# Layer 1 projections: the last key chunk's stores queued behind the last norm powers, and the eighth weight block's splits queued behind evictions

## The chip, the cores and the metric

The kernel runs as one launch on one core of a Trainium2 chip. The metric is the device time of one execution in microseconds (us), the median of several runs. The engines named here are TensorE (PE, matmuls; PEld its weight loads), VectorE (DVE), ScalarE (ACT), GpSimd (POOL) and SyncE (SP, which here only issues DMAs). Each engine runs its own list of instructions in order, and waits at an instruction until the semaphores that it names have been raised by other engines or by DMAs that have landed.

## The reference

A two-layer backbone works on T = 2304 tokens, 256 of context and 2048 latent ones on a grid of 32 rows and 64 columns, with D = 1024 channels. Layer 0 has two groups of heads, latent attention and bidirectional gated linear attention. Layer 1, in which the change lies, is a two-dimensional neighbourhood attention over 16 heads of 64. Cut to what matters:

```python
def odd_mixer(h, hc, w_in, q_gain, k_gain, rpb, w_out, update_ctx):   # layer 1; h: latent, hc: context tokens
    def heads(u):
        q, k, v, z = jnp.split(u, 4, axis=-1)
        return rms_norm(sh(q), q_gain), rms_norm(sh(k), k_gain), sh(v), z   # sh: 16 heads of 64
    q_x, k_x, v_x, z_x = heads(jnp.dot(h, w_in))
    q_c, k_c, v_c, z_c = heads(jnp.dot(hc, w_in))
    o = neighborhood_attention(q_x, k_x, v_x, k_c, v_c, rpb)   # windows of 8 rows x 16 columns, and the context
    y = jnp.dot(o.reshape(h.shape[0], h.shape[1], C_WIDTH) * jax.nn.silu(z_x), w_out)
    ...
```

So layer 1 needs the product of all token tiles with a 1024 x 4096 weight, and an RMS norm of every head of q and k. The kernel keeps k in two layouts: `K1`, from which it finds the maxima of the score rows, and `K1t`, which the attention itself reads later.

## The kernel before, in words

**Tiles and blocks.** Tokens are 18 tiles of 128 (tiles 0 and 1 are the context). The weight `w_od` is eight blocks of 512 columns: 0 and 1 are q, 2 and 3 are k, 4 and 5 are v, 6 and 7 are the gate z. One *cell* (t, j) multiplies tile t by block j: `mm3_steps` (L124) splits each fp32 factor into a high and a low part and makes three products (L129, L130, L131) for each of eight slices of D, 24 matmuls of 128 x 512, into a PSUM tile `gm`.

**Weights.** Four places w0 to w3 in SBUF hold the blocks: 2 and 4 share w0, 3 and 5 w1, 0 and 6 w2, 1 and 7 w3. A block is brought by `od_steps` (L1115) with `split_steps` (loop at L383): eight loads `wraw` of 256 KB by SP (L388) through a few staging buffers, each split into a high part by ACT (`w0h` to `w3h`, the activation of L106) and a low part by DVE (`w0l` to `w3l`, L391). When the last cell of blocks 2, 3, 0, 1 is through, `done(j)` appends block 4, 5, 6, 7 to the list `self.ahead`, from which `pump` takes a step at every fourth matmul step.

**Stage odd_qk (L1122)** runs q and k: cells in the order j = 2, 3, 0, 1 for each tile, the last two tiles (16 and 17) together, so that it ends (16,2), (17,2), (16,3), (17,3), (16,0), (17,0), (16,1), (17,1), and then (16,4), (17,4), the first two cells of v. Behind each q or k cell stands the norm: squares on ACT (`osq`), sums on DVE (`oss`, L1156), scale and power -1/2 on POOL (`rpow`, L208 and L210), the product on DVE (`onat`, L1159). A later cell's sixth step then calls `fin` (L1163): four PE transposes into `tp` (L1167), `oqh` and `oql` from them, stores to K (`K1`) or Q by SP. For k, `fin` also fills `okt`, the second layout in high and low parts, a chunk of 512 tokens (four tiles) at a time; when a chunk's last tile is in, `store_k` (L1196) issues four stores of 512 KB from POOL to `K1t` (L1200), for j = 2 and for j = 3. The last chunk's eight stores so stand on POOL among the powers of tiles 16 and 17. The two v cells evict to `onat` by ACT (L1150) and store to V1 from POOL (`store_v`, L1215, DMA at L1222).

**Stage odd_vz (L1224)** runs the rest of v and z with the tiles reversed: (17,5), (16,5), (17,6), (16,6), (17,7), (16,7), (15,4) and so on. Its pools take over memory that odd_qk's pools gave back. Block 5's cells evict to `ovz` by ACT and store to V1; z's are a tanh on ACT, a product on DVE (`ovz`, L1248) and PE transposes (L1251). Woven into them is `maxes`, row maxima of the scores per head: a key tile `mk` (1152 KB, from K), a table `mtab` (899 KB) to which POOL adds two masks (L1279, L1280), a query piece `mq`, spread by ACT into `mz` (zeroed by DVE, L1260), matmuls into `mx`, and reductions on DVE into `mm` (set by L1282).

**Order.** A framework orders each engine's instructions by its own forecast of a timeline. `issue_after(ins)` adds to that: what is issued inside it, on the same engine as `ins`, comes behind `ins`. `held(steps)` (L158) runs steps inside `issue_after(self.evicted.ins)`, so that ACT splits come behind the eviction kept in `self.evicted`. DMAs issued from POOL share one queue, and the compiled program takes eight completion counters in turn for them: a DMA waits for the one that used its counter before, eight DMAs earlier.

Of the kernel before, what the change touches and what calls it, by code (L numbers as in the profile page):

```python
# [13 lines left out]
ALU = mybir.AluOpType  # L14
# [7 lines left out]
CTX = 256  # L22
T = SEQ + CTX
NT = T // P
NCT = CTX // P
EPS = 1e-6
# [62 lines left out]
class Kern:  # L89
# [115 lines left out]
    def rpow(self, out, in_, mul, add):  # L205

        g = self.nc.gpsimd
        g.tensor_scalar(out=out, in0=in_, scalar1=mul, scalar2=add, op0=ALU.mult, op1=ALU.add)  # L208
        shp = list(out.shape)
        g.tensor_tensor(out=out, in0=out, in1=self.mhalf[:, : shp[1]], op=ALU.pow)  # L210


    def consts(self, es):
# [908 lines left out]
    def odd_qk(self, ws, win, hT):  # L1122
        nc = self.nc
        self.V1c = self.scr("V1c", (2, P, NCT, 512), F32)
        self.V1 = self.scr("V1", (2, SEQ, 512), F32)
        self.Q1 = self.scr("Q1", (2, 8, P, SEQ), F32)
        self.K1 = self.scr("K1", (8, P, T), F32)
        self.K1t = self.scr("K1t", (8, 2, P, T), F32)
        with ExitStack() as es:
            sp = self.pool(es, "osA", bufs=2, side="left", reuse_waits="tile")  # L1130
            pp = self.pool(es, "opA", bufs=2, space=PSUM, reuse_waits="tile")
            qkg = self.tl(sp, [P, 2], "oqkg", bufs=1)
            nc.sync.dma_start(qkg[:], self.i["od_gain"])
            nc.vector.tensor_scalar(out=qkg[:, 0:1], in0=qkg[:, 0:1], scalar1=0.125, scalar2=None, op0=ALU.mult)
            self.ahead += [self.od_steps(win, 0, ws), self.od_steps(win, 1, ws)]
            pend, kt = [], {}

            def cell(t, j):
                hi, lo = hT[t]
                wh, wl = win[j]  # L1140
                ps = self.tl(pp, [P, 8, 64], "gm", bufs=3)
                steps = self.mm3_steps(ps[:], (lambda k: hi[:, k, :], lambda k: lo[:, k, :]),
                                       (lambda k: wh[:, k, :], lambda k: wl[:, k, :]), range(KD))
                for n, _ in enumerate(steps):
                    if n == 5 and pend and (len(pend) > 1 or j == 4):
                        fin(*pend.pop(0))
                    yield
                if j == 4:
                    n = self.tl(sp, [P, 512], "onat", bufs=4)
                    self.act(n[:], ps[:].rearrange("p h d -> p (h d)"))  # L1150
                    self.store_v(t, 0, n)
                    return
                sq = self.tl(sp, [P, 512], "osq")
                self.act(sq[:], ps[:].rearrange("p h d -> p (h d)"), AF.Square)
                ss = self.tl(sp, [P, 8], "oss", bufs=4)
                nc.vector.tensor_reduce(out=ss[:], in_=sq[:].rearrange("p (h d) -> p h d", h=8), axis=AX.X, op=ALU.add)  # L1156
                self.rpow(ss[:], ss[:], 1.0 / 64, EPS)
                n = self.tl(sp, [P, 512], "onat", bufs=4)
                nc.vector.tensor_tensor(out=n[:].rearrange("p (h d) -> p h d", h=8), in0=ps[:],  # L1159
                                        in1=ss[:].unsqueeze(2).to_broadcast([P, 8, 64]), op=ALU.mult)  # L1160
                pend.append((t, j, n))

            def fin(t, j, n):  # L1163
                z = j // 2
                ps = self.tl(pp, [P, 4, P], "tp")
                for i in range(4):
                    nc.tensor.transpose(ps[:, i, :], n[:, i * P : i * P + P], self.ident[:])  # L1167
                hi = self.tl(sp, [P, 4, P], "oqh", F32R)
                self.act(hi[:], ps[:], AF.Copy, scale=qkg[:, z : z + 1])
                j0 = (j % 2) * 4  # L1170
                if z == 1:
                    nc.sync.dma_start(self.K1[j0 : j0 + 4, :, t * P : t * P + P].rearrange("j p t -> p j t"), hi[:].bitcast(F32))
                if z == 0 or t < NCT:
                    lo = self.tl(sp, [P, 4, P], "oql", F32R)
                    nc.vector.scalar_tensor_tensor(out=lo[:], in0=ps[:], scalar=qkg[:, z : z + 1], in1=hi[:],
                                                   op0=ALU.mult, op1=ALU.subtract)
                    if z == 0:
                        for part, tt in enumerate((hi, lo)):
                            nc.sync.dma_start(self.Q1[part][j0 : j0 + 4, :, (t - NCT) * P : (t - NCT) * P + P].rearrange("j p t -> p j t"),
                                              tt[:].bitcast(F32))  # L1180
                    else:
                        store_k((hi, lo), j0, t * P, P)
                    return
                g, r0 = divmod(2 * (t - NCT), 8)
                if r0 == 0:
                    kt[j] = [self.tl(sp, [P, 4, 512], f"okt{j}{part}", F32R, bufs=1) for part in range(2)]
                view = lambda x, n: x[:].rearrange("p i (r c b) -> p i r c b", r=n, c=4)
                for r in range(2):
                    oh, ol = (x[:].rearrange("p i (c b r) -> p i r c b", c=4, r=8)[:, :, r0 + r] for x in kt[j])
                    self.act(oh, view(ps, 2)[:, :, r], AF.Copy, scale=qkg[:, z : z + 1])  # L1190
                    nc.vector.scalar_tensor_tensor(out=ol, in0=view(ps, 2)[:, :, r], scalar=qkg[:, z : z + 1],
                                                   in1=view(hi, 2)[:, :, r], op0=ALU.mult, op1=ALU.subtract)
                if r0 == 6:
                    store_k(kt.pop(j), j0, CTX + g * 512, 512)

            def store_k(parts, j0, o, w):  # L1196

                for u, x in enumerate(parts):
                    for i in range(2):
                        nc.gpsimd.dma_start(self.K1t[j0 : j0 + 4, i, u * 64 : u * 64 + 64, o : o + w].rearrange("j d t -> d j t"),  # L1200
                                            x[i * 64 : i * 64 + 64].bitcast(F32))

            nxt = {2: 4, 3: 5, 0: 6, 1: 7}
            done = lambda j: j in nxt and self.ahead.append(self.od_steps(win, nxt[j], ws))
            cells = self.cells(list(range(NT)), (2, 3, 0, 1), lambda t, j: j > 1 or t >= NCT) + [(NT - 2, 4), (NT - 1, 4)]
            for _ in self.stream(cells, hT, cell, lambda t: self.prep(1, t, self.x1, pp, ("px", 2)), done):
                self.pump()
            while pend:
                fin(*pend.pop(0))
# [14 lines left out]
    def odd_vz(self, ws, win, hT):  # L1224
# [4 lines left out]
        with ExitStack() as es:  # L1229
# [6 lines left out]
            def cell(t, j):  # L1236
                hi, lo = hT[t]
                wh, wl = win[j]
                ps = self.tl(pp, [P, 512], "gm")
                yield from self.mm3_steps(ps[:], (lambda k: hi[:, k, :], lambda k: lo[:, k, :]),  # L1240
                                          (lambda k: wh[:, k, :], lambda k: wl[:, k, :]), range(KD))
                n = self.tl(sp, [P, 512], "ovz", bufs=3)
                if j < 6:
                    self.act(n[:], ps[:])
                    self.store_v(t, j - 4, n)
                    return
                self.last_tanh = self.act(n[:], ps[:], AF.Tanh, scale=0.5)
                nc.vector.scalar_tensor_tensor(out=n[:], in0=n[:], scalar=1.0, in1=ps[:], op0=ALU.add, op1=ALU.mult)  # L1248
                pt = self.tl(pp, [P, 4, P], "tp", bufs=1)
                for i in range(4):  # L1250
                    nc.tensor.transpose(pt[:, i, :], n[:, i * P : i * P + P], self.ident[:])  # L1251
                z = self.tl(sp, [P, 4, P], "ozt", bufs=1)
                self.act(z[:], pt[:])
                o = (t - NCT) * P
                nc.scalar.dma_start(self.z1[(j - 6) * 4 : (j - 6) * 4 + 4, :, o : o + P].rearrange("j p t -> p j t"), z[:])
# [61 lines left out]

            cells = self.cells(list(range(NT))[::-1], (4, 5, 6, 7), lambda t, j: (j > 4 or t < NT - 2) and (j < 6 or t >= NCT))
            gemms = self.stream(cells, hT, cell, lambda t: self.reload(1, t))
            self.weave(gemms, maxes(), 0.57, 15)  # L1320

# [415 lines left out]
```

## Time and profile before

| what | us |
|---|---|
| median of 3 runs | 3652.93 |
| lowest, highest | 3652.69, 3655.3 |
| the profiled execution | 3652.31 |
| its span, first to last instruction | 3650.5 |
| mean granted TensorE clock, share of full | 0.988 |

The profiled execution is 1.8 us longer than its span, and 0.6 us shorter than the median. In the rows of the profile a line number is that of the kernel; a time at the start of a row is counted from the start of the span; a bracket at the end, such as [1.94 <-DVE onat L1159], tells how long the engine had been idle before and what released it. A row of the waits reads: engine and operation that waited, what it waited for, us in total, times, longest. The stages of the change lie at about 2560 to 2850 us.

### The profile page before, as it was taken

What the parts mean: (1) busy time and instruction counts of PE and PEld (TensorE: products, weight loads), DVE (VectorE), ACT (ScalarE), POOL (GpSimd) and SP (SyncE); (2) the same over time, 40 slices, a digit from 0 to 9 for tenths busy, and PEclk for the clock granted to TensorE, in tenths of its full rate; (3) what the DMA queues carried; (4) which work ended last, traced back from release to release, by engine and by line L of the source; (5) the groups of instructions that cost most, each with busy time, mean ns of one, the idle gap of its engine ahead of it and who ended that gap; (6) DMA issues with size and microseconds to landing.
All of it is one profiled execution on the core that took longest, in us unless ns stands there. A gap on an engine that the chain in (4) does not pass through costs nothing. (4 is left out here: it accounts for less than half of the span.)

```text
span 3650.5 us, 51811 instructions
## 1 busy us (share of the span) xinstructions
PE 3552.0 (97%) x18404; PEld 2747.6 (75%) x18404; DVE 2355.2 (65%) x4846; ACT 1433.2 (39%) x2740; POOL 1234.9 (34%) x1376
## 2 busy tenths in 40 slices
PE   8999999999999999999999999999899999999899
PEld 6988987888886666665656887888788887555577
DVE  4677666888876766678765435455488784666732
ACT  5445551111115555555654214444422222555510
POOL 1433330101011211221311224333344442888763
PEclk9999999999999999999999999999999999999999
DMA  7455463222243232342632544545734446898672
GB/s 259 142 156 155 135 177 110 87 75 84 69 116 86 66 107 66 89 125 66 179 110 93 184 139 141 159 146 155 245 126 144 131 133 181 212 223 220 190 235 97
DMA packets 365780, 512.25 MB, mean 140 GB/s; under 512 B 26081, under 2 KB 245297, under 8 KB 359618
## 3 DMA queue, kind: packets, MB, share of 16 engines
q1 hardware_dynamic: 320754, 417.69, 39.3%
q0 software_dynamic: 22112, 63.26, 5.7%
q10 hardware_dynamic: 22656, 27.99, 2.2%
q8 instruction: 146, 2.39, 0.3%
q14 instruction: 112, 0.92, 0.1%
HBM read 329.45 MB, written 179.37 MB: 139 GB/s over the span
## 5 line engine op out<-in xcount | busy, mean ns | idle before, releaser
L963 DVE TENSOR_TENSOR acc<-acc,apt 128x512 f32<-128x512 f32 x512 | 375.6, 756 | 168.5 <-ACT apt L106 165.6
L106 ACT ACTIVATE apt<-st 128x512 f32<-128x512 f32 (+1 forms) x592 | 343.6, 594 | 290.7 <-PE st L974 262.0
L660 DVE TENSOR_REDUCE mm<-mx 128x1 f32<-128x512 f32 (+1 forms) x656 | 388.7, 629 | 87.3 <-PE mx L659 80.0
L914 PE MATMUL av<-apt,av 128*64 128x512 f32 (+1 forms) x1184 | 280.6, 594 | 0.0
L972 PE MATMUL st<-aq,akh 97*128 97x512 f32 (+1 forms) x592 | 256.6, 434 | 8.8 <-DMA aq<-QT 4.4
L659 PE MATMUL mx<-mk,mq 96*128 96x512 f32 (+1 forms) x656 | 235.8, 373 | 5.0 <-DMA mq<-QT 3.4
L1430 POOL TENSOR_TENSOR oacc<-oacc,opt 128x576 f32<-128x576 f32 (+5 forms) x192 | 223.0, 1184 | 39.7 <-ACT rl L106 19.3
L973 PE MATMUL st<-aq,akh 96*128 96x512 f32 (+1 forms) x592 | 235.5, 398 | 0.0
L1548 DVE TENSOR_TENSOR opt<-st,tab 128x64 f32<-128x64 f32 (+10 forms) x576 | 144.6, 317 | 140.3 <-PE st L1391 63.8
L974 PE MATMUL st<-aq,akl 96*128 96x512 f32 (+1 forms) x592 | 234.4, 396 | 0.0
L106 ACT ACTIVATE u<-gm 128x352 f32<-128x352 f32 (+1 forms) x140 | 68.6, 498 | 373.2 <-PE gm L131 210.6
L1307 DVE CUSTOM_DVE_ANT_1 mx<-mx,mtab 128x217 f32<-128x217 f32 (+12 forms) x576 | 184.2, 338 | 40.1 <-PE mx L1301 30.9
L914 PEld LDWEIGHTS av<-apt,av 128*64 128x64 f32 x1184 | 80.5, 137 | 153.6 <-issue 152.3
L972 PEld LDWEIGHTS st<-aq,akh 97*128 97x128 f32 x592 | 113.0, 191 | 99.1 <-issue 50.5
L106 ACT ACTIVATE opt<-opt 128x930 f32<-128x930 f32 (+7 forms) x129 | 104.2, 810 | 110.7 <-DVE opt L1548 102.6
L659 PEld LDWEIGHTS mx<-mk,mq 96*128 96x128 f32 x656 | 121.2, 188 | 16.8 <-DMA mk<-KT 3.8
L974 PEld LDWEIGHTS st<-aq,akl 96*128 96x128 f32 x592 | 113.9, 193 | 25.6
L973 PEld LDWEIGHTS st<-aq,akh 96*128 96x128 f32 x592 | 114.4, 193 | 17.1
L129 PE MATMUL gm<-w1h,hhi 128*128 128x512 f32 x288 | 116.3, 404 | 6.8 <-ACT onat L106 6.8
L106 ACT ACTIVATE x<-px,modB,modA 128x128 f32<-128x128 f32 x272 | 99.3, 468 | 56.9 <-PE px L339 54.4
L129 PE MATMUL gm<-w0h,hhi 128*128 128x512 f32 x288 | 116.3, 404 | 2.0 <-DVE hhi L351 1.9
L807 POOL TENSOR_TENSOR gsf<-gsf,D 64x512 f32<-64x512 f32 x17 | 25.1, 1477 | 271.4 <-DVE D L784 271.4
(492 smaller groups left out, 9962.1 us busy)
## 6 DMA issues: line engine op xcount, KB each, us to landing
q<-Q SPq DMA_DIRECT2D x48, 512.0 KB
H<-x ACTq DMA_DIRECT2D x36, 512.0 KB
adaw<-ada_w SPq DMA_DIRECT2D x64, 256.0 KB
x<-H SPq DMA_DIRECT2D x32, 512.0 KB
wraw<-w_od SPq DMA_DIRECT2D x64, 256.0 KB
K1t<-okt POOLq DMA_DIRECT2D x32, 512.0 KB, 7.6
kt<-K1t SPq DMA_DIRECT2D x32, 512.0 KB
mtab<-rpb_q SPq DMA_DIRECT2D x16, 899.0 KB
```

Source lines behind the costliest of these rows:

```text
L106: return self.nc.scalar.activation(out, in_, func, **kw)
L129: self.nc.tensor.matmul(out, lh(k), rh(k), start=j == 0, stop=False)
L659: mm = nc.tensor.matmul(ps[:, :w], q[:A_QK, (t % 6) * P : (t % 6) * P + P], k[:A_QK, k0 : k0 + w], start=True, stop=True)
L660: nc.vector.tensor_reduce(out=m[:, t, n : n + 1], in_=ps[:, :w], axis=AX.X, op=ALU.max)
L914: nc.tensor.matmul(O[j, nb][i * 64 : i * 64 + 64, :w], V[j, kt // TT][:, kt % TT, i * 64 : i * 64 + 64], pts[i][:, :w], start=n == 0, stop ...
L963: nc.vector.tensor_tensor(out=acc[i][:, :w], in0=a[:, :w], in1=pts[i][:, :w], op=ALU.add)
L972: nc.tensor.matmul(ps[:, :w], kh[: A_QK + 1, i, kq], qh[: A_QK + 1, :w], start=True, stop=False)
L973: nc.tensor.matmul(ps[:, :w], kh[:A_QK, i, kq], ql[:A_QK, :w], start=False, stop=False)
L974: mm = nc.tensor.matmul(ps[:, :w], kl[:A_QK, i, kq], qh[:A_QK, :w], start=False, stop=True)
L1307: nc.vector.tensor_tensor_reduce(out=s, in0=s, in1=tb[:, ri : ri + rn, ci : ci + cn], scale=1.0, scalar=-3e38, op0=ALU.add, op1=ALU.max, a ...
L1430: self.psum = nc.gpsimd.tensor_tensor(out=a, in0=a, in1=pts[:, :, a0 - r0 : a1 - r0, :], op=ALU.add)
L1548: bias = nc.vector.tensor_tensor(out=pt[:, d[0], d[1]], in0=ps[:, d[0], d[1]], in1=tabs[j][i][:, ri : ri + rn, ci : ci + cn], op=ALU.add)
```

## The change

`rpow` returns its power instruction. In odd_qk the stores of a key chunk are put into a list `last`; for the first three chunks they are issued at once, as before; the last chunk's eight (j = 2 and j = 3) wait in the list until cell (17,1), the last one with a norm, and are issued behind that cell's power on POOL. The evictions of v cells, in both stages, are now kept in `self.evicted`. Block 7, the eighth, is appended as `late()`: four empty steps, and then its loads and splits inside `held`, so that the splits on ACT come behind the eviction that is the last one when they are issued.

```diff
@@ rpow
-        g.tensor_tensor(out=out, in0=out, in1=self.mhalf[:, : shp[1]], op=ALU.pow)
+        return g.tensor_tensor(out=out, in0=out, in1=self.mhalf[:, : shp[1]], op=ALU.pow)
@@ odd_qk
-            pend, kt = [], {}
+            pend, kt, last = [], {}, []
@@ odd_qk, cell
-                    self.act(n[:], ps[:].rearrange("p h d -> p (h d)"))
+                    self.evicted = self.act(n[:], ps[:].rearrange("p h d -> p (h d)"))
...
-                self.rpow(ss[:], ss[:], 1.0 / 64, EPS)
+                power = self.rpow(ss[:], ss[:], 1.0 / 64, EPS)
...
                 pend.append((t, j, n))
+                if (t, j) == (NT - 1, 1):
+                    with self.tc.issue_after(power.ins):
+                        for x in last:
+                            store_k(*x)
@@ odd_qk, fin
                 if r0 == 6:
-                    store_k(kt.pop(j), j0, CTX + g * 512, 512)
+                    last.append((kt.pop(j), j0, CTX + g * 512, 512))
+                    if g < 3:
+                        store_k(*last.pop())
@@ odd_qk
+            def late():
+                yield from range(4)
+                yield from self.held(self.od_steps(win, 7, ws))
+
             nxt = {2: 4, 3: 5, 0: 6, 1: 7}
-            done = lambda j: j in nxt and self.ahead.append(self.od_steps(win, nxt[j], ws))
+            done = lambda j: j in nxt and self.ahead.append(late() if j == 1 else self.od_steps(win, nxt[j], ws))
@@ odd_vz, cell
                 if j < 6:
-                    self.act(n[:], ps[:])
+                    self.evicted = self.act(n[:], ps[:])
```

In the order of instructions that comes of it, the engines differ up to the end of the row maxima's first tables as follows. POOL: the last powers stand ahead of the eight K1t issues, then come the four V1 stores of `onat`, four of `ovz`, and the mask adds. ACT: all eight w2h splits stand ahead of the squares of (17,1) and of both `onat` evictions; four w3h splits stand between the eviction of (17,4) and that of (17,5), two more ahead of that of (16,5). DVE: two w2l splits stand ahead of the product of (17,0), six ahead of that of (16,1), all eight ahead of that of (17,1); the memsets of `mz` and `mm` stand ahead of the fifth to seventh w3l split. SP: the eighth load of block 7 stands behind `mk`, `mtab` and `mq`. The first seven `mx` matmuls on PE stand behind the first z transposes, and PE's other transposes move by at most six matmuls.

## The prediction

> **What bounds the kernel now.** I read the page's busy times, then PE's waits over the whole span, then the windows and timelines of the engines around the change.
>
> ```profile
> PE 3552.0 (97%) x18404; PEld 2747.6 (75%) x18404; DVE 2355.2 (65%) x4846; ACT 1433.2 (39%) x2740; POOL 1234.9 (34%) x1376
> ```
>
> TensorE is the bound: 97% busy. An edit that leaves its matmuls alone can win only where it stands still or runs at a lower clock. Its waits inside 2560 to 2720 us, where the change lies:
>
> ```profile
> PE gm L129 <- ACT onat L106: 6.8, 1, 6.8
> PE tp L1167 <- DVE onat L1159: 1.9, 1, 1.9
> PE tp L1251 <- DVE ovz L1248: 1.0, 1, 1.0
> PE mx L1301 <- DVE mm L1307: 0.6, 1, 0.6
> PE mx L1294 <- ACT mz L106: 0.6, 1, 0.6
> PE tp L1251 <- ACT mz L106: 0.2, 1, 0.2
> ```
>
> Six stalls, 11.1 us. Their places on PE's timeline, and three windows (columns: stretch, length, busy PE, PEld, DVE, ACT, POOL, granted clock, DMA share, GB/s):
>
> ```profile
> 2600.10 0.78 PE L1167 MATMUL tp<-ident,onat 128*128 128x128 f32 x4 [1.94 <-DVE onat L1159]
> ...
> 2613.59 0.39 PE L130 MATMUL gm<-w0l,hhi 128*128 128x512 f32 x1
> 2613.82 0.40 PE L131 MATMUL gm<-w0h,hlo 128*128 128x512 f32 x1
> 2620.98 0.79 PE L129 MATMUL gm<-w1h,hhi 128*128 128x512 f32 x1 [6.77 <-ACT onat L106]
> ...
> 2600.00:2605.00 5.00, 4.90 (x17) 4.04 (x18) 1.86 (x4) 1.70 (x3) 1.23 (x1) 0.66 1.06 318
> 2615.00:2620.00 5.00, 0.00 (x0) 0.00 (x0) 2.16 (x4) 2.02 (x4) 0.00 (x0) 0.75 0.91 286
> 2620.00:2625.00 5.00, 4.02 (x11) 3.23 (x12) 2.19 (x4) 2.08 (x4) 1.04 (x2) 0.57 0.91 264
> ```
>
> The two long stalls cost more than themselves: behind each the granted clock falls. 5.00 x (1 - 0.66) = 1.7 us are lost in the first window; 5.00 x (1 - 0.57) = 2.15 in the last, less 0.5 because PE stood idle for its first 0.98 us: again 1.7. (In 2615 to 2620 PE had nothing to run.) So the zone now loses 11.1 + 1.7 + 1.7 = **14.5 us**. That is the most that the change can take away.
>
> **Why the stalls are there.** POOL first, then the splits of block 6 (tile w2) and the eviction that PE waits for:
>
> ```profile
> 2594.59 1.31 POOL L1200 DMA_DIRECT2D K1t<-okt  x2 [9.11 <-ACT okt L106]
> 2595.97 0.26 POOL L208 TENSOR_SCALAR oss<-oss 128x8 f32<-128x8 f32 x1
> 2596.28 1.26 POOL L1200 DMA_DIRECT2D K1t<-okt  x2
> 2597.56 1.67 POOL L210 TENSOR_TENSOR oss<-oss,mhalf 128x8 f32<-128x8 f32 x1
> ...
> 2605.40 1.64 POOL L210 TENSOR_TENSOR oss<-oss,mhalf 128x8 f32<-128x8 f32 x1
> ...
> 2602.48 0.63 ACT L106 ACTIVATE w2h<-wraw 128x512 fp32r<-128x512 f32 x1 [5.35 <-DMA wraw<-w_od]
> ...
> L106 ACT ACTIVATE w2h<-wraw x8: 629/630/632, 2602.5 to 2619.8; 128x512 fp32r<-128x512 f32 x8
>   DMA wraw<-w_od: 15.5, 7
> ...
> 2620.35 0.58 ACT L106 ACTIVATE onat<-gm 128x512 f32<-128x512 f32 x1
> ```
>
> The 1.94 us stall waits for a norm's power that stands behind K1t issues (1.31 + 1.26 = 2.57 us of POOL, after POOL had itself waited 9.11 us for okt). The 6.77 us stall waits for the last onat eviction, queued on ACT behind all eight w2h splits; those come 17.3 / 7 = 2.5 us apart because they wait for their loads (15.5 us in 7 waits). An earlier block, with no K1t store in flight, was split faster:
>
> ```profile
> 2568.05 1.66 ACT L106 ACTIVATE w0h<-wraw 128x512 fp32r<-128x512 f32 x3
> 2572.26 1.18 ACT L106 ACTIVATE w0h<-wraw 128x512 fp32r<-128x512 f32 x2
> 2574.58 0.63 ACT L106 ACTIVATE w0h<-wraw 128x512 fp32r<-128x512 f32 x1 [1.15 <-DMA wraw<-w_od]
> 2576.69 1.25 ACT L106 ACTIVATE w0h<-wraw 128x512 fp32r<-128x512 f32 x2
> ```
>
> Eight splits in 9.9 us, 1.25 us each.
>
> **The change, part by part.** *Gain.* With the last chunk's eight stores behind the last power, no power waits for an issue: 2.57 us less in front of a 1.94 us stall, which goes, with its clock loss. In the new order, two w2l splits now stand in front of the product on VectorE, so I keep 0.5 us (0 to 1.9). With loads at 1.25 instead of 2.5 us and the first one's wait of 5.35 gone, the last w2h split starts at 2602.48 - 5.35 + 7 x 1.25 = 2605.9, before the last cell (17,4) ends. That cell ends at 2613.82 + 0.40 = 2614.2 now, and then at 2614.2 - 1.9 - 1.7 + 0.5 = 2611.1. What is late next is the eviction itself: 0.58 us and the handover, 1.0 us. Cell (17,5) so starts at 2612.1 instead of 2620.98. Holding block 7 behind evictions moves its w3h splits behind that eviction; PE reads w3 first in (17,7), four cells later, so I cost this at nothing. Its cover is those four cells; without it each split adds 0.63 us. PE's own order changes by transposes that move up to six matmuls: nothing, since they are ready.
>
> *What is given back.* The eight stores (4 MB) are now issued back to back on POOL, 8 x 0.64 = 5.1 us from the end of the last power, 2605.40 + 1.64 - 3.1 = 2603.9. How long do they take to land?
>
> ```profile
> DMA to landing us min/median/max: 4.5/7.5/11.7
> 2494.59 1.31 POOL L1200 DMA_DIRECT2D K1t<-okt  x2 [3.12 <-ACT okt L106]
> 2502.97 2.92 POOL L1200 DMA_DIRECT2D K1t<-okt  x4
> V<-onat POOLq DMA_DIRECT2D x2, 128.0 KB, 4.3
> ```
>
> The present groups of four: first issue 2594.59, last about 2596.9, landing up to 11.7 us later, so 2 MB take 14 us with weight loads beside; twice that is 28. The chunk before: first issue 2494.59, last about 2505.3, landing some 10 to 11.7 later, so eight stores take 21 to 22, with few loads beside. Here the w3 loads, Q stores and V stores run beside: I take 26 (nearer to the pair of groups), and the last lands at X = 2630, between 2626 and 2632.
>
> Who waits? All V stores of POOL come behind the eight on the same queue and reuse their eight completion counters, so V<-onat land only after X. A quarter of a store's bytes each, so a quarter of 26 / 8: 0.8 us apart. Tile (16,4)'s pair lands at X + 1.7 = 2631.7. The ACT eviction of (16,5) reuses onat's memory and waits for it; (16,6) needs that eviction's PSUM buffer (two gm buffers). PE's pace is 0.23 us a matmul (2613.59 to 2613.82), 24 of them 5.5 us a cell, so (16,6) is wanted at 2612.1 + 3 x 5.5 = 2628.6, and gets its buffer at 2631.7 + 0.6 = 2632.3: **3.7 us** stall (0 to 5.7), and a clock loss of 1.7 like behind the stalls above.
>
> By the Trainium skill (TensorE: Matmul & The Clock Gate, "What's actually happening") the clock falls only after an idle window of about 3.4 us. The trace differs: the 1.94 us stall was followed by a granted clock of 0.66. With that rule the sum would lose two of its three clock terms below, 3.4 us, and give 3650.8.
>
> Next is the product that PE transposes first in the z stage. VectorE, POOL and SP there:
>
> ```profile
> 2627.61 1.02 DVE L1260 MEMSET mz<- 64x512 f32 x2 [0.16 <-issue]
> 2629.74 0.62 DVE L391 TENSOR_TENSOR w3l<-wraw,w3h 128x512 fp32r<-128x512 f32 x1
> 2644.22 2.61 DVE L391 TENSOR_TENSOR w3l<-wraw,w3h 128x512 fp32r<-128x512 f32 x1 [12.53 <-ACT w3h L106]
> 2629.01 0.33 SPq L1278 DMA_DIRECT2D mtab<-rpb_q  x1
> 2629.43 0.59 SPq L1288 DMA_DIRECT2D mq<-Q  x1
> 2639.16 3.21 POOL L1279 TENSOR_TENSOR mtab<-mtab,maskq 128x1798 f32<-128x1798 f32 x1 [3.37 <-DMA mtab<-rpb_q]
> 2640.28 0.63 ACT L106 ACTIVATE mz<-mq 64x512 fp32r<-64x512 f32 x1 [5.82 <-DMA mq<-Q]
> 2647.48 0.66 PE L1251 MATMUL tp<-ident,ovz 128*128 128x128 f32 x4 [0.96 <-DVE ovz L1248]
> ```
>
> The mz memsets reuse memory that the last V<-onat still reads (X + 3.3 = 2633.3), and the order now puts them, some 2.2 us in all, ahead of three w3l splits: done at 2637.4 at 0.62 each. A split beside a POOL mask add took 2.61. The mtab load waits for a K1t store landing near X - 3 and was added to 10.1 us after its issue (2629.01 to 2639.16), so the adds begin near 2637: one to three of the splits are slow. The product of (17,6), 0.7 us, is ready at 2638 to 2644. PE wants it 2647.48 - 2620.98 = 26.5 us after (17,5)'s start, less 1.7 of clock, 1.5 of stalls, and some 1.4 for the seven mx matmuls now behind it: 21.9; so at 2612.1 + 21.9 + 3.7 + 1.7 = 2639.4. Stall 0 to 5, I take **2.5**, with 1.7 of clock. Last, SP: mk, mtab and mq each wait there for a K1t store, mq for the last one; behind them only w3's eighth load is queued. The mq load is issued at X, its mz split 10.9 us later (2629.43 to 2640.28), 2641, about when PE comes to it. But the max reductions share VectorE with the eighth w3l split and the POOL adds, as in the 2.61 row, and now begin closer together: **3.0** (0 to 5), and 1.7 of clock.
>
> *Sum.* After: 0.5 + 1.0 + 3.7 + 1.7 + 2.5 + 1.7 + 3.0 + 1.7 = 15.8 us lost, against 14.5: +1.3. The profiled run took 3652.31 (span 3650.5 and 1.8 around it), so 3653.6; it lies 0.6 under the median of the runs, 3652.93. Against that median: **3654.2 us**. In the attention stage that follows, only a few neighbours in an engine's order change places: nothing, give or take 2 us, no more than the small waits shown here.
>
> **The rivals.** *The stalls go and nothing comes back.* If the eight stores land within 15 us, by 2619, neither V<-onat nor the memsets are late. Left are 0.5 + 1.0 and up to 2 at the max reductions: 14.5 - 3.5 = 11 us faster, 3642. For it: DMA shares of 0.91 say the engines are not full. Against: no eight stores on the page took under 21. By the Trainium skill (DMA: Bandwidth & Descriptors, "Anatomy of one DMA — SWDGE (gpsimd) path") a store takes 2.0 us plus its bytes over 436 GB/s, which makes 11.6 us of 4 MB, and this rival; the trace's 14 us for 2 MB speaks against it. Chance 0.13.
>
> *The late drain decides.* With 28 us and another 2 for the mk and mtab loads, X is 2634: (16,6) stalls 7.7, all three w3l splits run at 2.6 beside the adds, so the product comes at 2634 + 3.3 + 2.2 + 7.8 + 0.7 = 2648.0 against 2643.4 wanted: 4.6; mq lands past 2645, 4.5; three clock losses 5.1; 1.5 remain. 23.4 - 14.5 = +9, 3662. It is slower by over 0.2% from X = 2633 on. For it: DMA is at 0.9 in this stretch already, bytes are only moved. Chance 0.20.
>
> *The eviction stays late.* If w2's loads keep 2.5 us because Q stores, not K1t, slow them, the last w2h split starts at 2602.48 - 5.35 + 17.3 = 2614.4 and the eviction after it ends at 2615.6, so (17,5) starts 3.7 us later than above; but then (16,6), which waits for X, stalls that much less. Only a clock loss of 1.7 is added: 3656, within 0.2%. Chance 0.07.
>
> **The numbers.** 0.2% is 7.3 us, about what a measurement of this kernel can tell from no change (its three runs span 2.6). The forecast itself, 0.60, with X from 2626 to 2632 and its terms at their ends, lies between 3646 and 3660. Faster is the first rival, 0.13; slower the second, 0.20; the rest 0.67. The range reaches to both: 3643 to 3663.
>
> **What would show it.** Right: the gaps at 2600 and before (17,5) gone or under 1.5 us, w2h splits 1.3 to 1.6 us apart; V<-onat landing after 2628; a gap before (16,6) ended by ACT's eviction, then one at L1251 ended by VectorE, each with a lower granted clock. Wrong: stores landing by 2620, or a gap before (17,5) of more than 3 us, or gaps that open after 2700.

## The result and the profile after

The changed kernel took 3659.25 us in the median of 20 runs (3654.05 to 3669.93), the kernel before 3654.10 in 20 runs beside them (3650.21 to 3663.81). The ratio is 1.0014 with a 95% interval of 1.0008 to 1.0021: slower by 2.9 to 7.7 us. The median's 0.14% is inside the 0.2% that was forecast, and above the forecast's +1.3 us.

PE's waits between 2570 and 2720 us in the changed kernel (engine and line, what it waited for, us in total, times, longest):

```profile
PE gm L129 <- ACT ovz L106: 11.2, 1, 11.2
PE mx L1304 <- ACT mz L106: 1.6, 1, 1.6
PE gm L129 <- ACT onat L106: 0.7, 1, 0.7
PE mx L1311 <- DVE mm L1317: 0.5, 1, 0.5
```

Six gaps of 11.1 us have become four of 14.0. The gap at the power is gone, that before (17,5) fell from 6.77 to 0.69, and one new gap of 11.2 us stands before (17,6). PE's timeline in the changed kernel, and three of its windows (the eighth column is the granted clock, the ninth the DMA share):

```profile
2612.74 0.50 PE L129 MATMUL gm<-w1h,hhi 128*128 128x512 f32 x1 [0.69 <-ACT onat L106]
2635.21 0.80 PE L129 MATMUL gm<-w2h,hhi 128*128 128x512 f32 x1 [11.20 <-ACT ovz L106]
2648.40 0.39 PE L1304 MATMUL mx<-mk,mz 128*128 128x256 f32 x1 [1.56 <-ACT mz L106]
...
2630.00:2635.00 5.00, 0.00 (x0) 0.00 (x0) 0.29 (x1) 0.96 (x2) 0.00 (x0) 0.50 0.25 88
2635.00:2640.00 5.00, 4.79 (x12) 3.85 (x13) 4.03 (x10) 2.69 (x6) 2.06 (x4) 0.55 0.67 159
2640.00:2645.00 5.00, 5.00 (x23) 4.09 (x23) 1.02 (x2) 1.50 (x2) 0.00 (x0) 1.00 0.98 404
```

(17,5) starts 8.2 us earlier than before (2612.74 against 2620.98), and the new gap takes that back and more. Behind it the clock is halved: 5.00 x (1 - 0.55) = 2.25 us, less 0.1 because PE stood idle for the first 0.21 us. So the stretch loses 14.0 + 2.15 = 16.2 us, against 14.5 before.

Why (17,6) waits so long is read on ACT, POOL and SP of the changed kernel (the w2h rows are read further below):

```profile
2593.23 0.63 ACT L106 ACTIVATE w2h<-wraw 128x512 fp32r<-128x512 f32 x1 [0.91 <-DMA wraw<-w_od]
2602.06 1.29 ACT L106 ACTIVATE w2h<-wraw 128x512 fp32r<-128x512 f32 x2 [2.46 <-DMA wraw<-w_od]
2603.82 0.62 ACT L106 ACTIVATE w2h<-wraw 128x512 fp32r<-128x512 f32 x1
2604.34 0.59 ACT L106 ACTIVATE osq<-gm 128x512 f32<-128x512 f32 x1
...
2612.59 1.66 ACT L106 ACTIVATE w3h<-wraw 128x512 fp32r<-128x512 f32 x3
2634.04 0.63 ACT L106 ACTIVATE w3h<-wraw 128x512 fp32r<-128x512 f32 x1 [19.79 <-DMA wraw<-w_od]
2634.58 0.58 ACT L106 ACTIVATE ovz<-gm 128x512 f32<-128x512 f32 x1
...
2608.42 5.08 POOL L1206 DMA_DIRECT2D K1t<-okt  x8
...
2613.96 21.79 SPq L388 DMA_DIRECT2D wraw<-w_od  x4
DMA to landing us min/median/max: 4.6/11.1/16.6
```

The eviction of (17,5), on which (17,6) waits for its PSUM buffer, stands on ACT behind the fourth w3h split. That split waited 19.79 us for a load issued at 2613.96 (the first of the four in the SP row), while the eight stores were in flight (the last row is for K1t<-okt). Their last one, issued near 2612.9, landed 16.6 us later, at 2629.5. The load came another 4.5 us after that, though the DMA engines were busy for only 0.25 of 2630 to 2635 (the first window above); why its last packets took so long stays open.

A length that doesn't depend on what runs did elsewhere: from the matmul that waits 1.87 us for `hhi`, ahead of the stretch, to the first transpose of `mc`, behind it, from start to start. In the kernel before, in a second profile of it, in the changed kernel and in a second profile of that one:

```profile
2557.16 0.50 PE L129 MATMUL gm<-w0h,hhi 128*128 128x512 f32 x1 [1.87 <-DVE hhi L351]
2679.79 0.27 PE L1264 MATMUL mx<-ident,mc 128*16 128x128 f32 x1
```

```profile
2555.68 0.50 PE L129 MATMUL gm<-w0h,hhi 128*128 128x512 f32 x1 [1.87 <-DVE hhi L351]
2677.43 0.27 PE L1264 MATMUL mx<-ident,mc 128*16 128x128 f32 x1
```

```profile
2556.87 0.50 PE L129 MATMUL gm<-w0h,hhi 128*128 128x512 f32 x1 [1.87 <-DVE hhi L351]
2682.61 0.27 PE L1274 MATMUL mx<-ident,mc 128*16 128x128 f32 x1
```

```profile
2555.11 0.50 PE L129 MATMUL gm<-w0h,hhi 128*128 128x512 f32 x1 [1.87 <-DVE hhi L351]
2679.48 0.27 PE L1274 MATMUL mx<-ident,mc 128*16 128x128 f32 x1
```

Before 122.63 and 121.75, after 125.74 and 124.37: longer by 2.9 us in the mean (1.7 to 4.0). The mean spans differ by the same 2.9 (3655.5 and 3650.5 after, 3650.5 and 3649.7 before). The medians' 5.15 is more, but their interval begins at 2.9; no place was found for the rest.

### The profile page after: what moved, and what is told of

Read it like the earlier page. It is cut to its first block, busy times and chain, and to the rows that moved or that the text cites. A ratio compares the mean times of both kernels' runs of the same rounds, so it can differ in the third digit from the quotient of the medians.

```text
span 3655.5 us, 51807 instructions
## 1 busy us (share of the span) xinstructions
PE 3555.6 (97%) x18404; PEld 2753.7 (75%) x18404; DVE 2352.9 (64%) x4846; ACT 1431.3 (39%) x2740; POOL 1231.0 (34%) x1376
## 4 chain that ended last, share of the span: by engine, by line
PE 83%; DMA 6%; DVE 5%; POOL 2%; ACT 2%; issue 2%; SPq 0%; DVEq 0%; ACTq 0%; POOLq 0%
PE gm L129 10%; PE gm L130 10%; PE gm L131 10%; PE av L914 6%; PE st L972 4%; PE mx L659 4%; PE st L973 3%; PE st L974 3%; PE st L1400 2%; PE o L1434 2%; PE pj L129 2%; PE pj L131 2%; PE pj L130 2%; PE st L129 2%; PE st L131 2%; PE st L130 2%
## 5 line engine op out<-in xcount | busy, mean ns | idle before, releaser
L659 PEld LDWEIGHTS mx<-mk,mq 96*128 96x128 f32 x656 | 121.9, 189 | 16.2 <-issue 5.4
```

The source lines that it names most:

```text
L659: mm = nc.tensor.matmul(ps[:, :w], q[:A_QK, (t % 6) * P : (t % 6) * P + P], k[:A_QK, k0 : k0 + w], start=True, stop=True)
```

## The experiments

Theory A: the split in front of the eviction, and its load caught in the heap of stores, are the whole fault. Theory B: the forecast's wait, V stores that land late. Theory C, formed after the first four: the stretch is short of DMA time, and an order only chooses which load PE waits for. Each set shares its own runs of the kernel before; not all sets ran on the same chip. "The stretch" is the length just defined, in the one profile of each kernel; the two profiles of one kernel above differ by 0.9 and 1.4 us.

**Only the held splits.** The stores at their old places:

```diff
-                if (t, j) == (NT - 1, 1):
-                    with self.tc.issue_after(power.ins):
-                        ...
-                    last.append((kt.pop(j), j0, CTX + g * 512, 512))
-                    ...
+                    store_k(kt.pop(j), j0, CTX + g * 512, 512)
```

> Only the second half of the change: block 7's splits held behind evictions, the last chunk's K1t stores at their old places among the powers. Theory A (the eight stores in one heap starve SP's queue, where block 7's fourth load stands behind Q stores; its split then blocks the eviction of (17,5) on ACT): no gap of 11 us before (17,6); the gaps at the power (1.9 us) and before (17,5) (5 to 7 us) are back, since w2's loads still run beside K1t; within 3 us of the kernel before. Theory B (the forecast: V stores land late and the eviction of (16,5) waits for their memory): also no late gap, within 3 us of before.

3661.49 us against 3657.19 (ratio 1.0010, 1.0001 to 1.0020); stretch 127.95. Both theories expected it within 3 us of the kernel before; the medians are 4.3 apart. Both old gaps are back, as expected, but a third is there. Its waits, and VectorE and POOL ahead of that third gap:

```profile
PE gm L129 <- ACT onat L106: 6.7, 1, 6.7
PE tp L1255 <- DVE ovz L1252: 4.3, 1, 4.3
...
2655.42 6.80 DVE L391 TENSOR_TENSOR w3l<-wraw,w3h 128x512 fp32r<-128x512 f32 x2 [2.32 <-ACT w3h L106]
2653.88 7.78 POOL L1284 TENSOR_TENSOR mtab<-mtab,maskq 128x1798 f32<-128x1798 f32 x2
```

Two w3l splits beside POOL's mask adds took 6.8 us together, ahead of the product of z. Held splits alone move work into that time; alone they don't help.

**Only the stores.** Block 7 as before:

```diff
-            done = lambda j: j in nxt and self.ahead.append(late() if j == 1 else self.od_steps(win, nxt[j], ws))
+            done = lambda j: j in nxt and self.ahead.append(self.od_steps(win, nxt[j], ws))
```

> Only the first half: the eight K1t stores behind the last power, block 7 split as in the kernel before, so that most w3h splits stand on ACT ahead of the two onat evictions. Theory A: the fourth w3h split waits some 20 us for its load and now stands ahead of the onat evictions, so the gap moves to before (17,5) and is 15 us or longer; 5 to 12 us slower than before. Theory B: ACT's order does not matter for it, a gap of 2 to 6 us before (16,6) ended by V stores; within 4 us of before.

3666.46 us (1.0026, 1.0014 to 1.0037), the worst but one; stretch 131.33. PE's wait, and the split (here the seventh) and the eviction on ACT that end it:

```profile
PE gm L129 <- ACT onat L106: 19.8, 1, 19.8
...
2635.58 0.63 ACT L106 ACTIVATE w3h<-wraw 128x512 fp32r<-128x512 f32 x1 [9.56 <-DMA wraw<-w_od]
2636.12 0.58 ACT L106 ACTIVATE onat<-gm 128x512 f32<-128x512 f32 x1
```

The gap moves with the split, as A says and B doesn't: where the late splits stand on ACT decides which eviction PE misses.

**Six empty steps instead of four.**

```diff
-                yield from range(4)
+                yield from range(6)
```

> The whole change, but six empty steps instead of four, which puts the fourth and later w3h splits behind the evictions of (17,5) and (16,5) on ACT. K1t stores as in the change. Theory A: the 11.2 us gap goes; what is left is the eviction of (16,5) waiting for V stores until about 2631, a gap of 2 to 3 us before (16,6) with one clock loss; 6 to 10 us faster than the change, 3 to 7 faster than before. Theory B: the split was not the cause, and (17,6) starts no earlier than in the change (about 2635); within 3 us of the change.

3665.46 us (1.0025, 1.0016 to 1.0035); stretch 130.39. PE's waits and ACT:

```profile
PE mx L1304 <- ACT mz L106: 7.1, 1, 7.1
PE mx L1311 <- DVE mm L1317: 3.5, 2, 2.9
PE tp L1261 <- DVE ovz L1258: 2.4, 2, 1.4
PE gm L129 <- ACT ovz L106: 1.9, 1, 1.9
...
2630.80 0.60 ACT L106 ACTIVATE ovz<-gm 128x512 f32<-128x512 f32 x1 [10.00 <-DMA V<-onat]
```

The 11.2 us gap went, and what was left before (16,6) is the forecast's wait, at half its price: (16,5)'s eviction waits for V stores until 2630.80, 1.9 us of PE. The gain expected of A did not come: 7.1 us at mx, for an mq that SP had issued only at 2633.84, and smaller ones. So A names the cause of the gap and not the price.

**Half the heap.** The stores of j = 2 at once:

```diff
-                    if g < 3:
+                    if g < 3 or j == 2:
```

> The whole change, but only the four stores of j = 3 wait for the last power; the four of j = 2 are issued when their tile is full, as before. Theory A: with 2 MB instead of 4 behind the last power, K1t is through near 2620 and the fourth w3 load near 2623, so the eviction of (17,5) is late by at most 1 us against (17,6) wanted near 2624; the gap shrinks from 11.2 to under 2 us; 6 to 11 us faster than the change. Theory B: V stores land near 2622, no gap either; the same time.

3662.98 us (1.0017, 1.0008 to 1.0026); stretch 126.71. A expected less than 2 us before (17,6), and that was missed: it still waited 5.2 us, for the eviction behind the fourth split (its load had come by 2634.89, 15.3 us after (17,5)'s start at 2619.61, against 21.3 in the change), and z's transposes waited 5.3 for the product. Half a heap makes the split six microseconds earlier and lets the next wait show.

**Block 7's loads on ACT's queue.**

```diff
-                self.wload = nc.sync.dma_start(w[:], src[:, s, c])
+                self.wload = (nc.scalar if tag == "w3" and key == 7 else nc.sync).dma_start(w[:], src[:, s, c])
```

> The whole change; only block 7's eight loads are issued from ACT, on ACT's own DMA queue, and no longer on SP's behind the Q stores. Theory A1 (the fourth load is late because it stands in SP's queue behind Q stores, which crawl beside K1t): it lands within 10 us of its issue instead of 20, the gap of 11.2 us before (17,6) ends near 2627 to 2631 instead of 2635, where V stores take over as in the run with six empty steps. Theory A2 (all queues share the engines, and nothing issued in that time lands before K1t is through, near 2630): the fourth load lands at 2628 or later and the gap stays over 9 us.

3662.66 us against 3654.72 (1.0020, 1.0011 to 1.0029); stretch 125.75. ACT's queue and ACT, around the fourth load:

```profile
2621.05 0.33 ACTq L388 DMA_DIRECT2D wraw<-w_od  x1
...
2624.09 0.63 ACT L106 ACTIVATE w3h<-wraw 128x512 fp32r<-128x512 f32 x1 [1.48 <-DMA wraw<-w_od]
2624.62 0.58 ACT L106 ACTIVATE ovz<-gm 128x512 f32<-128x512 f32 x1
2629.74 0.63 ACT L106 ACTIVATE w3h<-wraw 128x512 fp32r<-128x512 f32 x1 [4.54 <-DMA wraw<-w_od]
```

The load took 8.7 us (2621.05 to 2629.74) instead of 20. It was also issued later in the backlog, 15.2 us after the first K1t store instead of 5.5, so these two times alone don't decide. The queues between 2615 and 2622 do, in the changed kernel and, behind the dots, in this one (packets, MB, share of 16 engines; q0 is POOL's queue, q1 SP's, q10 ACT's):

```profile
q0 software_dynamic: 574, 2.09, 88.7%
q1 hardware_dynamic: 574, 0.29, 14.0%
...
q0 software_dynamic: 444, 1.62, 65.0%
q10 hardware_dynamic: 396, 0.73, 27.2%
q1 hardware_dynamic: 446, 0.22, 10.6%
```

The queues get about as many packets as each other, but those of SP are of 0.5 KB, the rows of the Q stores: in the change the weight load behind them has moved next to nothing in that time. ACT's queue moves 1.8 KB a packet. So A1 holds: on SP the load stood behind Q stores of 256 KB. By the Trainium skill (DMA: Bandwidth & Descriptors, "Queues, rings and completion order") an engine goes round the queues that have work, a packet at a time; these rows agree.

The gap before (17,6) fell to 3.8 us, but 5.7 at mx and 2.5 at the product came in its place. The order on ACT is another one here, too: three splits, not four, stand ahead of (17,5)'s eviction (2624.62), and the third held it. And the profiled run, 3654.49, is the fastest of its ten, 8.2 us under their median, so this profile doesn't show the whole price.

**Maxima three cells later.**

```diff
-            self.weave(gemms, maxes(), 0.57, 15)
+            self.weave(gemms, maxes(), 0.57, 15, 24)
```

> The whole change, and the row maxima begin 24 matmul steps (three cells) later, so that mk, mtab and mq are wanted some 17 us later. Theory A: the 11.2 us gap, which stands ahead of them, stays; the 2.1 us at mx go; 2 to 4 us faster than the change. Theory C (the stretch is short of DMA time as a whole, and each order only chooses which load PE waits for): with less wanted before 2650, the loads of w3 and the V stores come no sooner, the gap before (17,6) stays within 2 us of 11.2, and no new gap takes the place of mx; the same 2 to 4 us.

3666.48 us (1.0031, 1.0022 to 1.0041); 2 to 4 us less than the change had been expected. The gap before (17,6) is 10.5 and the mx gaps are gone, as expected; the end of the stage pays, where PE now waits for the attention's queries:

```profile
PE gm L129 <- ACT ovz L106: 10.5, 1, 10.5
...
PE st L1400 <- DMA q<-Q: 9.1, 1, 9.1
```

**Both kernels once more**, for a second profile (the rows are above):

> The kernel before once more, for a second profile: the same six gaps between 2598 and 2655, about 14.5 us with their clock losses, within 2 us; other places may differ by as much as the runs do.

> The changed kernel once more, for a second profile: the gap of 11 us before (17,6) again, and about 16 us lost between 2598 and 2655, within 2 us. If the loss differs by more, the stretch itself varies from run to run.

In the kernel before again, the gaps before (17,5) and at the powers were 7.3 and 2.3 us, but the clock was not halved near 2600. Its windows:

```profile
2600.00:2605.00 5.00, 5.00 (x27) 4.20 (x27) 2.15 (x4) 1.70 (x3) 1.30 (x2) 1.00 1.05 303
```

So 1.7 of the 14.5 us that the prediction counted as the old loss were chance. Counted in the same way, gaps and clock, this second profile loses 10.2 + 2.0 = 12.2 us, 2.3 less than expected. In the changed kernel again, the gap was 9.7 and the loss 11.8 + 2.9 = 14.7. The changed kernel so loses 1.7 us more in the first pair of profiles and 2.5 in the second.

**Loads ahead of the splits**, without and with later maxima. Block 7 is written out: its next load follows each split, and two empty steps stand ahead of the fourth split.

```diff
+                for n, ks in enumerate(((0, 1), (2,), (3, 4), (5, 6), (7,))):
+                    if n == 2:
+                        yield from range(2)
+                    for k in ks:
+                        part(k)             # split k, then load k + 3
+                    yield
```

> The whole change, but block 7's loads run ahead of its splits: six loads are queued on SP before mk, mtab and mq, as the change has it, while the fourth and later w3h splits stand on ACT behind the evictions of (17,5) and (16,5). Theory A: no gap of 11 us; the gap of about 2 us before (16,6) that V stores leave, then w3 in time. Theory C (short of DMA time as a whole): the mq load is not issued before 2632, so PE waits at mx, some 5 to 7 us as in the run with six empty steps; sum of gaps and clock losses 14 to 20 us, no faster than the change by more than 2.

> The same, and the row maxima begin 12 matmul steps later at a ratio of 0.6 instead of 0.57, so that they end no later than before. Theory C: the demand for mk, mtab and mq moves by some 8 us, behind the backlog; what is left is the gap before (16,6) and small ones, 4 to 8 us with clock losses; 5 to 10 us faster than the change, 2 to 7 faster than the kernel before, unless the end of the stage pays for it, as with 24 steps, where PE waited 9.1 us for the query tiles of the attention.

> The kernel before, only with the row maxima beginning 12 matmul steps later at a ratio of 0.6. Its two large gaps lie ahead of the maxima, so both theories expect them to stay; the small ones of 2.4 us behind them go: 0 to 2 us faster than before. If it is slower, the later start costs at the end of the stage, and that price is in the run before this one too.

3661.15 us against 3657.15 (1.0014, 1.0005 to 1.0024), 3660.34 (1.0013, 1.0004 to 1.0023), and 3658.36 for the kernel before with later maxima (1.0013, 1.0004 to 1.0022). The first left 2.3 us before (16,6), 2.4 at the product and 4.3 at mx (stretch 124.24): as C says, the loss goes to mx. In the last the small gaps behind 2640 are 0.5 us instead of 2.4, but in the second profile of the kernel before they are 0.6 without any edit. It is no faster: PE's waits behind 2700 sum to 23.1 us, against 19.9 and 21.3 in the two profiles of the kernel before, and to 26.8 in the second kernel. That the later start of the maxima causes these is likely, not shown. The gain expected of the second did not come either.

**Fewer bytes.** The low parts of the last key chunk and of the last two tiles' queries are stored earlier, from the tiles before. So 3 MB less move in the stretch, and these places hold other tiles' low parts:

```diff
-                    last.append((kt.pop(j), j0, CTX + g * 512, 512))
+                    last.append((kt.pop(j)[: 2 - g // 3], j0, CTX + g * 512, 512))
+                    if g == 2:
+                        store_k(last[-1][0], j0, CTX + 3 * 512, 512, (1,))
...
-                        for part, tt in enumerate((hi, lo)):
-                            nc.sync.dma_start(self.Q1[part][...(t - NCT)...], tt[:])
+                        for part, tt in enumerate((hi, lo)):
+                            for a in [t] if not part or t < NT - 4 else [t, t + 2] if t < NT - 2 else []:
+                                nc.sync.dma_start(self.Q1[part][...(a - NCT)...], tt[:])
```

> The whole change, with 3 MB less to move in the stretch: the low parts of the last key chunk (four of the eight stores) and of the last two tiles' queries (four Q stores of 256 KB) are left out there, and their places are filled earlier, some 15 to 100 us before, with the low parts of the tiles before them; so these places hold other low parts than the reference's. Orders on all engines stay as in the change. Theory C (the stretch is short of DMA time, at 0.27 MB per us): the backlog ends 3 / 0.27 = 11 us sooner, the last K1t store lands near 2619, the fourth w3 load near 2622, the gap of 11.2 us shrinks under 1 and the rest to 1 to 5; 8 to 13 us faster than the change, 4 to 9 faster than before. Theory A alone (the fault is the split that stands ahead of the eviction, whatever is behind it): the gap shrinks too, but the loss goes on to mx as in the run with six empty steps, and the time stays within 4 us of the change.

3658.07 us against 3654.88 (1.0005, 0.9995 to 1.0015): the only kernel not clearly slower. Its landmarks, waits, POOL and VectorE:

```profile
2558.51 0.67 PE L129 MATMUL gm<-w0h,hhi 128*128 128x512 f32 x1 [1.87 <-DVE hhi L351]
2679.50 0.27 PE L1277 MATMUL mx<-ident,mc 128*16 128x128 f32 x1
...
PE tp L1264 <- DVE ovz L1261: 6.6, 1, 6.6
PE mx L1307 <- ACT mz L106: 1.4, 1, 1.4
PE gm L129 <- ACT ovz L106: 1.2, 1, 1.2
...
2640.56 7.31 POOL L1293 TENSOR_TENSOR mtab<-mtab,maskq 128x1798 f32<-128x1798 f32 x2
2640.12 8.30 DVE L391 TENSOR_TENSOR w3l<-wraw,w3h 128x512 fp32r<-128x512 f32 x1 [2.12 <-ACT w3h L106]
```

The gap before (17,6) went from 11.2 to 1.2, with the same order on ACT: the backlog of stores makes the split late. The stretch is 120.99, 4 us shorter than the two of the change in the mean, not the 8 to 13 that C expected: one w3l split, 8.3 us long beside two mask adds, holds the product of z, and PE waits 6.6 us. So C falls in its pure form: behind the DMA backlog stands VectorE beside POOL, which takes back most of what the shorter gap gave. The stretch is shorter than the kernel before's (122.63 and 121.75), and the time still isn't: PE's waits behind 2700 sum to 24.3 us here, against 19.5 and 19.6 in the change. What makes them longer was not tested.

## Why the prediction was right, and where its steps failed

**The sign and size.** It said +1.3 within 3643 to 3663; measured +5.15 with 2.9 at the low end, and 3659.25. Its sum of losses after, 15.8, met 16.2 in the profile, but with other terms in it; that is partly luck.

**Right.** The gaps at the power and before (17,5) went for the reason given: w2h splits now 1.5 us apart (2593.23 to 2603.82, eight), (17,5) at 2612.74 where 2612.1 was forecast. The handover cost 0.7 us, not 1.0. V<-onat landed at about 2631, close to the forecast's 2631.7; the wait priced at 3.7 us shows in the run with six empty steps, as 1.9.

**Mis-sized, and cancelling.** The stores were to be issued "from the end of the last power, 2605.40 + 1.64 - 3.1 = 2603.9": it was 2608.42, because the squares of (17,1) stand on ACT behind the eight w2h splits, which had waited for loads (2.46 us ahead of 2602.06). "I take 26" for the flight: it took 21.1 (2608.42 to 2629.5), as the earlier chunk's row had said. The two errors, 4.5 us late and 4.9 us short, cancel, and X came to 2629.5 where 2630 was forecast: luck.

**Failed.** "Holding block 7 behind evictions moves its w3h splits behind that eviction; PE reads w3 first in (17,7), four cells later, so I cost this at nothing." It looked at the reader of w3, four cells on, and not at what stands behind the split on ACT. The fourth split waited 19.79 us and held the eviction of (17,5): 11.2 us of PE, in place of the 3.7 before (16,6) and the 2.5 at the product; at the row maxima 2.1 were lost, for the 3.0 forecast. What is queued behind a waiting instruction had been asked for SP and VectorE, and not for ACT.

**The clock.** Three losses of 1.7 were forecast behind three gaps; there was one of 2.2 behind the one long gap, and behind the 1.56 us at 2648.40 the granted clock stayed at 1.00. The 1.7 counted at 2600 in the old loss came in one of two profiles only.

**The rivals.** The stalls didn't just go: eight stores took 21 us, not under 15. The eviction did not stay late: w2's loads no longer came 2.5 us apart. The late drain at X = 2634 did not occur either, but its second half, the product held by w3l splits beside the mask adds, is what remained in three experiments (4.3, 5.3 and 6.6 us).

## What to carry to other kernels

When a DMA heap is moved, follow every load that is in flight with it to the engine that consumes it, and read what that engine has queued behind: a split with four cells of slack blocked an eviction with none. Where several waits lie within a few microseconds of each other, taking one away shows the next (here, stores, then mq, then VectorE beside POOL); work out the second before expecting the first one's full price. A sum of losses that comes out right can hold the wrong terms; only the gap's place and releaser tell.

## What the runs showed of the hardware

Between 2615 and 2622 of the changed kernel, POOL's queue and SP's moved 574 packets each, 2.09 MB against 0.29. A load of 256 KB that stood behind Q stores on SP's queue took 20 us there; one from ACT's own queue, issued later in such a backlog, took 8.7.

A 128 x 512 subtraction on VectorE, 0.69 us alone, took 1.8 to 8.3 us beside POOL adds of 128 x 1798. Such a split ended just behind the end of an add: at 2662.22 behind 2661.66 with only the held splits, at 2648.42 behind 2647.87 with fewer bytes. That is as if it had not been served while an add ran; no run isolates it. Reductions from PSUM beside such an add kept their 0.68 us.

A gap of 1.94 us ahead of 2600 was followed by 3.4 us at half clock in one profile of the kernel before (5.00 x (1 - 0.66) / 0.5), a gap of 1.74 us at the same place by none in the other. By the Trainium skill (TensorE: Matmul & The Clock Gate, "What's actually happening") the gate's window runs free of the kernel; that would fit, but no run here tests it.
